# Max-pool-and-subtract on one core: 48 KB tiles in four buffers, the last one in three shrinking pieces, no ScalarE

## Chip, cores and metric

The kernel runs on one core of a Trainium2 chip; the other cores are idle. The metric is the device time of one execution in microseconds (us); lower is better. A verdict of "same" means within 2%.

## The reference

```python
def setup_inputs():
    B, C, H, W = 8, 64, 256, 256
    return {"x": np.random.randn(B, C, H, W).astype(np.float32)}

def reference(x):
    ...   # pH = pW = 8
    x_r = x.reshape(B, C, oH, pH, oW, pW)
    pooled = x_r.max(axis=(3, 5))
    upsampled = np.repeat(np.repeat(pooled, pH, axis=2), pW, axis=3)
    return (x - upsampled).astype(np.float32)
```

From each 8 x 8 window its maximum is subtracted. 134.22 MB go in and 134.22 MB come out; each element is used once. In the kernels a "row" is 8 image lines of one channel, 2048 floats (8 KB) in one partition. 128 such rows, one per partition, are 1 MB, and "a tile of R rows" has R of them in each partition; the whole input is 128 rows deep.

## The kernel before

```python
    R = 2
    data_pool = ctx.enter_context(tc.tile_pool(name="data_pool", bufs=8))
    small_pool = ctx.enter_context(tc.tile_pool(name="small_pool", bufs=4))
    for i in range(ntiles):                      # 64 tiles
        dat = data_pool.tile([P, R, row_len], mybir.dt.float32, name="dat")
        nc.sync.dma_start(out=dat..., in_=src)   # load, cut here
        for r in range(R):
            nc.vector.tensor_reduce(out=pooled[:, r], in_=in_v, axis=XY, op=max)
        nc.scalar.activation(out=rep..., in_=pooled...to_broadcast(...), func=Copy)
        for r in range(R):
            nc.vector.tensor_tensor(out=dat_v, in0=dat_v,
                in1=rep[:, r].unsqueeze(1).to_broadcast([P, pH, W]), op=subtract)
        nc.scalar.dma_start(out=dst, in_=dat...)  # store
```

(Abridged.) Loads are issued from SP (queue q1), stores from the ScalarE sequencer (queue q10). A scheduler decided the order of instructions on each engine.

Of the kernel before, what the change touches and what calls it, by code (L numbers as in the profile page):

```python
# [1 line left out]

# [4 lines left out]


@with_exitstack  # L10
def kernel(
    ctx: ExitStack,
    tc: tile.TileContext,
    x: bass.AP,
    out: bass.AP,
):
    nc = tc.nc
    P = nc.NUM_PARTITIONS

    B, C, H, W = x.shape  # L20
    pH = pW = 8
    oH, oW = H // pH, W // pW

    x_rows = x.rearrange("b c (oh ph) w -> (b c oh) (ph w)", ph=pH)
    out_rows = out.rearrange("b c (oh ph) w -> (b c oh) (ph w)", ph=pH)
    n_rows = x_rows.shape[0]
    row_len = x_rows.shape[1]

    R = 2
    rows_per_tile = P * R  # L30
    ntiles = n_rows // rows_per_tile
    assert n_rows % rows_per_tile == 0

    data_pool = ctx.enter_context(tc.tile_pool(name="data_pool", bufs=8))
    small_pool = ctx.enter_context(tc.tile_pool(name="small_pool", bufs=4))

    for i in range(ntiles):
        dat = data_pool.tile([P, R, row_len], mybir.dt.float32, name="dat")
        src = x_rows[i * rows_per_tile : (i + 1) * rows_per_tile].rearrange(
            "(p r) d -> p (r d)", r=R  # L40
        )
        nc.sync.dma_start(out=dat.rearrange("p r d -> p (r d)"), in_=src)  # L42

        pooled = small_pool.tile([P, R, oW], mybir.dt.float32, name="pooled")
        rep = small_pool.tile([P, R, W], mybir.dt.float32, name="rep")

        for r in range(R):
            in_v = dat[:, r].rearrange("p (ph ow pw) -> p ow ph pw", ph=pH, ow=oW, pw=pW)
            nc.vector.tensor_reduce(  # L49
                out=pooled[:, r],  # L50
                in_=in_v,
                axis=mybir.AxisListType.XY,
                op=mybir.AluOpType.max,
            )

        nc.scalar.activation(  # L56
            out=rep.rearrange("p r (ow pw) -> p (r ow) pw", pw=pW),
            in_=pooled.rearrange("p r ow -> p (r ow)").to_broadcast([P, R * oW, pW]),
            func=mybir.ActivationFunctionType.Copy,
        )  # L60

        for r in range(R):
            dat_v = dat[:, r].rearrange("p (ph w) -> p ph w", ph=pH)
            nc.vector.tensor_tensor(  # L64
                out=dat_v,
                in0=dat_v,
                in1=rep[:, r].unsqueeze(1).to_broadcast([P, pH, W]),
                op=mybir.AluOpType.subtract,
            )

        dst = out_rows[i * rows_per_tile : (i + 1) * rows_per_tile].rearrange(
            "(p r) d -> p (r d)", r=R
        )
        nc.scalar.dma_start(out=dst, in_=dat.rearrange("p r d -> p (r d)"))  # L74


# [1 line left out]
_INS = ['x']  # L78
_OUTS = [((8, 64, 256, 256), 'float32')]


# [23 lines left out]
```

## Time and profile before

| | before |
|---|---|
| time, median of 3 runs | 631.79 us (631.71 to 631.91) |
| span of the profiled run | 630.3 us |
| VectorE (DVE) busy | 564.7 us, 90% |
| ScalarE (ACT) busy | 39.5 us, 6% |
| mean DMA rate | 426 GB/s |

Parts of the page of the kernel before: span, busy time, the DMA rows of the 40 time slices (busy tenths, then GB/s), the queues, the chain of waits, and the three large groups of instructions. A group's columns are line, engine, operation, output and input, count, then busy us and mean ns of one, then the idle time just before and what ended it.

```profile
span 630.3 us, 730 instructions
...
DVE 564.7 (90%) x256; ACT 39.5 (6%) x65; POOL 0.2 (0%) x4
...
DMA  9999999999999999999999999999999999999997
GB/s 361 418 433 433 432 431 432 428 431 433 431 428 433 432 432 433 433 431 432 431 429 431 433 432 428 432 432 431 433 433 431 433 429 429 431 433 433 431 405 334
...
q1 hardware_dynamic: 9216, 134.22, 50.0%
q10 hardware_dynamic: 9216, 134.22, 49.8%
...
DMA 81%; DVE 16%; issue 1%; DVEq 0%; ACT 0%; SPq 0%; ACTq 0%
...
L49 DVE TENSOR_REDUCE pooled<-dat 128x32 f32<-128x2048 f32 x128 | 285.0, 2276 | 57.6 <-DMA dat<-in_x_dram 57.6
L64 DVE TENSOR_TENSOR dat<-dat,rep 128x2048 f32<-128x2048 f32 x128 | 283.9, 2282 | 0.8 <-ACT rep L56 0.8
L56 ACT ACTIVATE rep<-pooled 128x512 f32<-128x512 f32 x64 | 38.2, 624 | 578.4 <-DMA dat<-in_x_dram 408.2
```

The DMA engines are full from end to end at about 431 GB/s; the two queues take half of them each. VectorE is busy for 90% and its only idle time of note is waiting for loads. ScalarE hardly delays anybody (0.8 us). What the engines do not use is at the two ends. The end of the kernel before, in windows of 4 us (us, DVE busy, ACT, POOL, clock, DMA share, GB/s), and then VectorE's instructions there (start, busy us, line, operation, count, idle before). A packet is counted in the window in which it starts, so a share can exceed 1.

```profile
608.00:612.00 4.00, 4.00 (x3) 0.00 (x0) 0.00 (x0) 1.00 0.78 332
612.00:616.00 4.00, 4.00 (x3) 0.00 (x0) 0.00 (x0) 1.00 1.07 455
616.00:620.00 4.00, 3.25 (x2) 0.63 (x1) 0.00 (x0) 1.00 0.95 406
620.00:624.00 4.00, 3.13 (x2) 0.00 (x0) 0.00 (x0) 1.00 0.47 201
624.00:628.00 4.00, 0.00 (x0) 0.00 (x0) 0.00 (x0) 1.00 1.08 459
```

```profile
604.60 2.29 DVE L49 TENSOR_REDUCE pooled<-dat 128x32 f32<-128x2048 f32 x1 [2.80 <-DMA dat<-in_x_dram]
606.80 8.88 DVE L64 TENSOR_TENSOR dat<-dat,rep 128x2048 f32<-128x2048 f32 x4
615.61 2.28 DVE L49 TENSOR_REDUCE pooled<-dat 128x32 f32<-128x2048 f32 x1
618.64 4.49 DVE L64 TENSOR_TENSOR dat<-dat,rep 128x2048 f32<-128x2048 f32 x2 [0.76 <-ACT rep L56]
```

VectorE gets the last tile at 604.6. It still has two earlier tiles to finish besides, so from 608 to 624 the store queue runs dry twice: a bubble of about 3 us.

### The profile page before, as it was taken

To read this page: it belongs to the slowest core of one execution; us is meant where nothing else is said; L and a number is where in the kernel's file an instruction comes from. 1 tells how busy PE (TensorE), PEld (TensorE's weight loads), DVE (VectorE), ACT (ScalarE), POOL (GpSimd) and SP (SyncE) were. 2 spreads that over 40 slices of the span, in tenths; PEclk is the share of its full clock that TensorE was granted. 3 is DMA by queue.
4 is the path that set the end of the run, shared out by engine and by line. 5 is a ranking of instruction groups with operands and counts; after the bars stand their busy time and mean duration, and the time that the engine had idled before them with its cause. 6 is when DMAs were issued, how large, how long until landed. Compare 5 with 4: busy or idle time off the path is not lost.

```text
span 630.3 us, 730 instructions
## 1 busy us (share of the span) xinstructions
DVE 564.7 (90%) x256; ACT 39.5 (6%) x65; POOL 0.2 (0%) x4
## 2 busy tenths in 40 slices
DVE  4999999889889889889889898898998988988985
ACT  1000010010000000000001001001001001001000
POOL 0000000000000000000000000000000000000000
DMA  9999999999999999999999999999999999999997
GB/s 361 418 433 433 432 431 432 428 431 433 431 428 433 432 432 433 433 431 432 431 429 431 433 432 428 432 432 431 433 433 431 433 429 429 431 433 433 431 405 334
DMA packets 18437, 268.48 MB, mean 426 GB/s; under 512 B 2048, under 2 KB 2048, under 8 KB 2048
## 3 DMA queue, kind: packets, MB, share of 16 engines
q1 hardware_dynamic: 9216, 134.22, 50.0%
q10 hardware_dynamic: 9216, 134.22, 49.8%
q14 instruction: 5, 0.04, 0.0%
HBM read 134.22 MB, written 134.22 MB: 426 GB/s over the span
## 4 chain that ended last, share of the span: by engine, by line
DMA 81%; DVE 16%; issue 1%; DVEq 0%; ACT 0%; SPq 0%; ACTq 0%
DMA dat<-in_x_dram 49%; DMA out_dram<-dat 32%; DVE dat L64 9%; DVE pooled L49 7%; DVEq L100 0%; ACT rep L56 0%; SPq L42 0%; ACTq L74 0%; DVEq L64 0%; ACTq L56 0%
## 5 line engine op out<-in xcount | busy, mean ns | idle before, releaser
L49 DVE TENSOR_REDUCE pooled<-dat 128x32 f32<-128x2048 f32 x128 | 285.0, 2276 | 57.6 <-DMA dat<-in_x_dram 57.6
L64 DVE TENSOR_TENSOR dat<-dat,rep 128x2048 f32<-128x2048 f32 x128 | 283.9, 2282 | 0.8 <-ACT rep L56 0.8
L56 ACT ACTIVATE rep<-pooled 128x512 f32<-128x512 f32 x64 | 38.2, 624 | 578.4 <-DMA dat<-in_x_dram 408.2
L56 ACT ACT_TABLE_LOAD x1 | 1.3, 1283 | 0.7 <-PEq L89 0.7
L89 POOL MEMSET const-uint8-127<- 128x1 uint8 x1 | 0.1, 103 | 0.0
L89 POOL MEMSET const-bfloat16-1.0<- 128x1 bf16 x1 | 0.1, 102 | 0.0
L89 POOL MEMSET const-float32-0.0<- 128x1 f32 x1 | 0.1, 99 | 0.2 <-issue 0.2
L89 POOL MEMSET const-float32-1.0<- 128x1 f32 x1 | 0.1, 99 | 0.0
## 6 DMA issues: line engine op xcount, KB each, us to landing
dat<-in_x_dram SPq DMA_DIRECT2D x64, 2048.0 KB, 29.6
out_dram<-dat ACTq DMA_DIRECT2D x64, 2048.0 KB, 19.0
```

Of the source, the lines that this page charges most:

```text
L49: nc.vector.tensor_reduce(out=pooled[:, r], in_=in_v, axis=mybir.AxisListType.XY, op=mybir.AluOpType.max,)
L56: nc.scalar.activation(out=rep.rearrange("p r (ow pw) -> p (r ow) pw", pw=pW), in_=pooled.rearrange("p r ow -> p (r ow)").to_broadcast([P, ...
L64: nc.vector.tensor_tensor(out=dat_v, in0=dat_v, in1=rep[:, r].unsqueeze(1).to_broadcast([P, pH, W]), op=mybir.AluOpType.subtract,)
L89: nc = _bacc.Bacc("TRN2", target_bir_lowering=False, num_devices=1)
```

## The change

Its intent: fewer and longer transfers (48 KB per partition instead of 16), less fixed cost per instruction (one reduction per tile, the subtraction reads the maxima directly), and a short end (the last tile comes in pieces of 3, 2 and 1 rows, so that little work is left after the last byte arrives). The order is that of the program. The core of the diff:

```diff
+TILES = [[2]] + [[6]] * 20 + [[3, 2, 1]]
+BUFS = 4
 ...
-        for r in range(R):
-            nc.vector.tensor_reduce(out=pooled[:, r], in_=in_v, ...)
-        nc.scalar.activation(out=rep..., in_=pooled...to_broadcast(...), func=Copy)
+            nc.vector.tensor_reduce(                      # one for all R rows
+                out=tops, in_=wins.rearrange("p r ph ow pw -> p r ow ph pw"), ...)
         for r in range(R):
             nc.vector.tensor_tensor(
-                in1=rep[:, r].unsqueeze(1).to_broadcast([P, pH, W]),
+                in1=tops[:, r].unsqueeze(1).unsqueeze(3).to_broadcast([P, pH, oW, pW]),
 ...
+    ctx.enter_context(tc.manual_schedule())
+    for pieces in TILES:
+        dat = data.tile([P, size * ROW], F32, name="dat")
+        for R in pieces:
+            src = x_rows[at : at + P * R].rearrange("(p r) d -> p (r d)", r=R)
+            dst = out_rows[at : at + P * R].rearrange("(p r) d -> p (r d)", r=R)
+            part = dat[:, done * ROW : (done + R) * ROW]
+            ...
+            nc.sync.dma_start(out=part, in_=src)
+        for part, tops, dst, R in parts:
+            pool_and_subtract(part, tops, R)
+            nc.scalar.dma_start(out=dst, in_=part)
```

More of the change, by code (lines that the diff above doesn't have):

```diff
@@ L7 @@
 from concourse._compat import with_exitstack
+F32 = mybir.dt.float32
+ROW = 2048
+TILES = [[2]] + [[6]] * 20 + [[3, 2, 1]]
+BUFS = 4
 @with_exitstack
@@ L21, with pool_and_subtract @@
     pH = pW = 8
-    oH, oW = H // pH, W // pW
+    oW = W // pW
     x_rows = x.rearrange("b c (oh ph) w -> (b c oh) (ph w)", ph=pH)
     out_rows = out.rearrange("b c (oh ph) w -> (b c oh) (ph w)", ph=pH)
-    n_rows = x_rows.shape[0]
-    row_len = x_rows.shape[1]
-    R = 2
-    rows_per_tile = P * R
-    ntiles = n_rows // rows_per_tile
-    assert n_rows % rows_per_tile == 0
-    data_pool = ctx.enter_context(tc.tile_pool(name="data_pool", bufs=8))
-    small_pool = ctx.enter_context(tc.tile_pool(name="small_pool", bufs=4))
-    for i in range(ntiles):
-        dat = data_pool.tile([P, R, row_len], mybir.dt.float32, name="dat")
-        src = x_rows[i * rows_per_tile : (i + 1) * rows_per_tile].rearrange(
-            "(p r) d -> p (r d)", r=R
-        )
-        nc.sync.dma_start(out=dat.rearrange("p r d -> p (r d)"), in_=src)
-        pooled = small_pool.tile([P, R, oW], mybir.dt.float32, name="pooled")
-        rep = small_pool.tile([P, R, W], mybir.dt.float32, name="rep")
-        for r in range(R):
-            in_v = dat[:, r].rearrange("p (ph ow pw) -> p ow ph pw", ph=pH, ow=oW, pw=pW)
+    assert sum(map(sum, TILES)) * P == x_rows.shape[0]
+    size = max(map(sum, TILES))
+    data = ctx.enter_context(tc.tile_pool(name="data", bufs=BUFS))
+    small = ctx.enter_context(tc.tile_pool(name="small", bufs=BUFS))
+    def pool_and_subtract(dat, tops, R):
+        wins = dat.rearrange("p (r ph ow pw) -> p r ph ow pw", r=R, ph=pH, ow=oW)
+        tops = tops.rearrange("p (r ow) -> p r ow", r=R)
+        if R == 1:
             nc.vector.tensor_reduce(
-                out=pooled[:, r],
-                in_=in_v,
+                out=tops[:, 0],
+                in_=wins[:, 0].rearrange("p ph ow pw -> p ow ph pw"),
                 axis=mybir.AxisListType.XY,
@@ L54 @@
             )
-        nc.scalar.activation(
-            out=rep.rearrange("p r (ow pw) -> p (r ow) pw", pw=pW),
-            in_=pooled.rearrange("p r ow -> p (r ow)").to_broadcast([P, R * oW, pW]),
-            func=mybir.ActivationFunctionType.Copy,
-        )
+        else:
+            nc.vector.tensor_reduce(
+                out=tops,
+                in_=wins.rearrange("p r ph ow pw -> p r ow ph pw"),
+                axis=mybir.AxisListType.XY,
+                op=mybir.AluOpType.max,
+            )
         for r in range(R):
-            dat_v = dat[:, r].rearrange("p (ph w) -> p ph w", ph=pH)
             nc.vector.tensor_tensor(
-                out=dat_v,
-                in0=dat_v,
-                in1=rep[:, r].unsqueeze(1).to_broadcast([P, pH, W]),
+                out=wins[:, r],
+                in0=wins[:, r],
+                in1=tops[:, r].unsqueeze(1).unsqueeze(3).to_broadcast([P, pH, oW, pW]),
                 op=mybir.AluOpType.subtract,
             )
-        dst = out_rows[i * rows_per_tile : (i + 1) * rows_per_tile].rearrange(
-            "(p r) d -> p (r d)", r=R
-        )
-        nc.scalar.dma_start(out=dst, in_=dat.rearrange("p r d -> p (r d)"))
+    ctx.enter_context(tc.manual_schedule())
+    at = 0
+    for pieces in TILES:
+        dat = data.tile([P, size * ROW], F32, name="dat")
+        pooled = small.tile([P, size * oW], F32, name="pooled")
+        parts = []
+        done = 0
+        for R in pieces:
+            src = x_rows[at : at + P * R].rearrange("(p r) d -> p (r d)", r=R)
+            dst = out_rows[at : at + P * R].rearrange("(p r) d -> p (r d)", r=R)
+            part = dat[:, done * ROW : (done + R) * ROW]
+            tops = pooled[:, done * oW : (done + R) * oW]
+            parts.append((part, tops, dst, R))
+            at += P * R
+            done += R
+            nc.sync.dma_start(out=part, in_=src)
+        for part, tops, dst, R in parts:
+            pool_and_subtract(part, tops, R)
+            nc.scalar.dma_start(out=dst, in_=part)
 _INS = ['x']
```

## The prediction

> **What bounds it now.** The DMA engines. In the page's slices DMA is at 9 in all but the last, at 428 to 433 GB/s from the third to the thirty-eighth. Every byte is needed, so at 431 GB/s moving alone takes 268.44 MB / 431 = 622.8 us of the 630.3 us span.[...] VectorE is second: 256 instructions (groups: mean 2276 and 2282 ns), 564.7 us busy, 4.4 us per row of 1 MB against 4.85 us of DMA for that row in and out. The chain (DMA 81%) alternates 29 us loads and 19 us stores: queueing behind busy engines, so shorter waits for buffers gain nothing.
>
> About 7.5 us isn't moving: 2.3 us until data flows, 1.5 us after the last byte, and a bubble of about 3 us at the end. In windows of 4 us the rate falls to 332 GB/s at 608 and 201 GB/s at 620: loads are over, and VectorE, two tiles behind, releases the last three stores at 611, 616 and 623 us.
>
> **What the change does.**
> - 128 DMAs of 2 MB become 48, most of 6 MB, in runs of 48 KB instead of 16 KB. Packets now are 16 KB and take about 0.61 us (queue table: 50.0% of 16 engines' span over 9216 packets, 1024 of them tiny)[...]. If runs are cut to 16 KB again, the gain is zero.
> - ScalarE's 64 copies (39.5 us, off the path; VectorE waited 0.8 us on them) vanish: under 1 us.
> - 128 reductions become 24; the fixed part of one is about 0.06 us, so VectorE saves about 6 us, off the path. Subtractions read maxima with step 0 inside; I expect 2.28 us still.
> - Coarser tiles: load 29, compute 26.4, store 29 us, together 85, against four tiles x 29 = 116 us per turn of buffers. Queues never run dry.
> - Start: the first tile is as before; 20 rows are requested up front instead of 16. No loss.
> - End: pieces of 3, 2, 1 rows; VectorE finishes the last row 4.4 us after it lands, while earlier pieces still drain. The 3 us bubble shrinks to about 0.5.
>
> **Sum.** 631.8 - 2.5 (end)[...] - 0.5 = 625.8 us. Range 623.2 to 629.4. Faster by over 2% needs 619.2[...]: 2%. Slower by over 2%: 3%.
>
> **What would show it.** Slices flat at 431 to 435 GB/s; far fewer packets, of 48 KB; the last slice above 370 GB/s; subtractions of 2.28 us; six-row reductions near 12.9 us; VectorE near 560 us; no wait of the load queue that takes DMA under 9.
>
> **What would make it wrong.** Subtractions over 2.6 us (VectorE would bind); packets still of 16 KB and 431 GB/s (then 628.5); a store queue dry early, or large store packets starving the small last loads, a bubble of several us.

The sum came to 625.8 us. One term is cut out of it, 3 us less for the longer packets (the author's estimate of 4 us, at three chances in four); the terms left give 628.8. The fixed 0.06 us of a reduction is what the traces show: 2.195 us from one reduction to the next before, less 2.133 us per further row within one after ("Why the prediction was wrong").

## The result

Here and below, a ratio is the mean time of one kernel's fast runs over the mean of the other's of the same rounds, so it is not quite the ratio of the medians quoted.

| | before | changed |
|---|---|---|
| median | 631.85 us (4 runs) | 631.81 us (4 runs) |
| lowest to highest | 631.71 to 631.91 | 630.37 to 634.03 |
| ratio | | 1.0004, 95% interval 0.9981 to 1.0027 |

No gain. The median lies above the predicted range, which ended at 629.4, and 6 us above the predicted 625.8. New is the scatter: before, runs agree within 0.2 us; after, they spread over 3.7 us, all at full clock.

The same parts of the page of the changed kernel (the groups are those with different shapes kept apart):

```profile
span 629.1 us, 305 instructions
...
DVE 560.0 (89%) x152; POOL 0.2 (0%) x4
...
DMA  9999999999999999999999999999999999999995
GB/s 383 430 403 450 444 406 444 450 406 444 447 406 447 444 409 447 447 406 447 444 416 438 447 419 434 447 428 425 447 431 422 444 438 422 444 419 430 439 423 252
...
q1 hardware_dynamic: 3456, 134.22, 49.6%
q10 hardware_dynamic: 3456, 134.22, 49.4%
...
another core or an unknown queue 51%; DVE 26%; DMA 19%; issue 1%; SPq 1%
...
dat<-in_x_dram SPq DMA_DIRECT2D x1, 1024.0 KB, 64.9
```

```profile
L55 DVE TENSOR_TENSOR dat<-dat,pooled 128x2048 f32<-128x2048 f32 x128 | 284.0, 2286 | 0.8
L48 DVE TENSOR_REDUCE pooled<-dat 128x192 f32<-128x12288 f32 x20 | 259.0, 12950 | 40.7 <-DMA dat<-in_x_dram 40.7
...
L41 DVE TENSOR_REDUCE pooled<-dat 128x32 f32<-128x2048 f32 x1 | 2.3, 2285 | 7.1 <-DMA dat<-in_x_dram 7.1
```

Much is as foreseen: VectorE has 560.0 us, subtractions take 2286 ns and six-row reductions 12.95 us, ScalarE has no work left, there are 3456 packets per queue instead of 9216. (The swing between 403 and 450 GB/s is how packets of 48 KB fall into slices of 15.7 us: 8 or 9 of them started per engine would make 400 or 450 GB/s, an estimate.) The half of the chain that names an unknown queue is not another core, since only one runs; the page could not match that DMA. Two lines do not fit. The last slice is at 252 GB/s where 370 was expected, and the last load of 1 MB took 64.9 us from issue to landing, with VectorE idle 7.1 us for it. The end, as for the kernel before (these windows have no ACT column):

```profile
608.00:612.00 4.00, 0.52 (x1) 0.00 (x0) 1.00 1.00 424
612.00:616.00 4.00, 0.42 (x1) 0.00 (x0) 1.00 0.99 426
616.00:620.00 4.00, 3.96 (x2) 0.00 (x0) 1.00 0.93 397
620.00:624.00 4.00, 0.19 (x1) 0.00 (x0) 1.00 0.72 299
624.00:628.00 4.00, 0.00 (x0) 0.00 (x0) 1.00 0.10 41
```

```profile
599.57 4.42 DVE L48 TENSOR_REDUCE pooled<-dat 128x64 f32<-128x4096 f32 x1 [2.96 <-DMA dat<-in_x_dram]
604.03 4.49 DVE L55 TENSOR_TENSOR dat<-dat,pooled 128x2048 f32<-128x2048 f32 x2
615.58 2.29 DVE L41 TENSOR_REDUCE pooled<-dat 128x32 f32<-128x2048 f32 x1 [7.06 <-DMA dat<-in_x_dram]
617.90 2.29 DVE L55 TENSOR_TENSOR dat<-dat,pooled 128x2048 f32<-128x2048 f32 x1
```

Most of the data is out by 624, which is 4 to 5 us sooner than before; yet the span ends at 629.1. In the window from 624 to 628 only 41 GB/s flow, about what one or two of the 16 DMA engines move (27.2 GB/s each by the packet durations below). So some engines were still at work when the others were done.

The trace shows this directly. Every DMA ends with 16 four-byte writes (1024 such packets for 64 DMAs on each queue before), called completion writes here. In the records of one engine, chained below, exactly one of them follows the eight data packets that this engine moves for a DMA (8 x 16 engines are the 128 partitions), and VectorE starts on the last load only after the last of its 16 (604.60 after 604.1 before, 615.58 after 615.2 changed). So each is read here as one engine's sign that its part is done. Sorted by time and taken by sixteens, they tell when the median engine and when the slowest engine finished (us from the start of the span, as in the profile; the first data packet starts at 1.7):

```
                        last load            last store
                     median  slowest       median  slowest
before                602.0    604.1        629.0    629.1
changed               609.7    615.2        623.7    628.0
changed, second run   lag 5.3               lag 4.3
```

("Lag" is slowest less median; the second run is the one of experiment 4.) The median engine gained 5.3 us, as hoped. The slowest engine trails by 4.3 us at the end, by 5.5 us at the last load, and the last row waits for the slowest (615.2; VectorE starts it at 615.58).

A packet, here and below, is one record of the trace: the bytes that one DMA moves for one partition, or one completion write. Durations give a clean law, by median: 8 KB takes 309 ns, 16 KB 611, 24 KB 912, 32 KB 1213, 40 KB 1514, 48 KB 1815. From 8 to 48 KB that is 1506 ns for 40,960 bytes, 27.2 GB/s per engine or 435 GB/s for 16, plus about 8 ns per packet. Data packets alone therefore take, per engine, 16384 x 611 / 16 = 625.7 us before and 619.9 us after (the same sum over its four lengths): 5.8 us less. The gain exists, and is lost elsewhere.

The records do not name their engine, but they can be chained: on one engine each record begins 3 to 4 ns before the one ahead of it ends. From the completion write that comes last in the changed kernel's trace (628.0), exactly one record fits at every step back to 207.0 us, 296 records without a gap. So the slowest engine never idles in that time. It is late because 13 of its packets each took over 50 ns more than the median of their length, 3.7 us together, where it trails by 4.3; the other slow packets lie on other engines or before 207 us. On it, packets of the two queues alternate one by one, 8 KB loads with 48 KB stores at the end: with the completion writes counted, the queue changes at each of the 271 steps up to the last load's completion write; where one queue comes twice in a row, the other's completion write had taken a turn between.

### The profile page after: what moved, and what is told of

It is laid out like the page before. It is cut to its first block, busy times and chain, and to the rows that moved or that the text cites. A ratio compares the mean times of both kernels' runs of the same rounds, so it can differ in the third digit from the quotient of the medians.

```text
span 629.1 us, 305 instructions
## 1 busy us (share of the span) xinstructions
DVE 560.0 (89%) x152; POOL 0.2 (0%) x4
## 3 DMA queue, kind: packets, MB, share of 16 engines
q1 hardware_dynamic: 3456, 134.22, 49.6%
q10 hardware_dynamic: 3456, 134.22, 49.4%
## 4 chain that ended last, share of the span: by engine, by line
another core or an unknown queue 51%; DVE 26%; DMA 19%; issue 1%; SPq 1%
DVE pooled L48 13%; DVE dat L55 13%; DMA dat<-in_x_dram 12%; DMA out_dram<-dat 8%; SPq L77 1%; DVE pooled L41 0%
## 5 line engine op out<-in xcount | busy, mean ns | idle before, releaser
L48 DVE TENSOR_REDUCE pooled<-dat 128x192 f32<-128x12288 f32 (+2 forms) x23 | 274.4, 11930 | 52.3 <-DMA dat<-in_x_dram 52.3
L55 DVE TENSOR_TENSOR dat<-dat,pooled 128x2048 f32<-128x2048 f32 x128 | 284.0, 2286 | 0.8
L41 DVE TENSOR_REDUCE pooled<-dat 128x32 f32<-128x2048 f32 x1 | 2.3, 2285 | 7.1 <-DMA dat<-in_x_dram 7.1
## 6 DMA issues: line engine op xcount, KB each, us to landing
dat<-in_x_dram SPq DMA_DIRECT2D x1, 1024.0 KB, 64.9
```

Of the source, the lines that this page charges most:

```text
L41: nc.vector.tensor_reduce(out=tops[:, 0], in_=wins[:, 0].rearrange("p ph ow pw -> p ow ph pw"), axis=mybir.AxisListType.XY, op=mybir.AluOp ...
L48: nc.vector.tensor_reduce(out=tops, in_=wins.rearrange("p r ph ow pw -> p r ow ph pw"), axis=mybir.AxisListType.XY, op=mybir.AluOpType.max,)
L55: nc.vector.tensor_tensor(out=wins[:, r], in0=wins[:, r], in1=tops[:, r].unsqueeze(1).unsqueeze(3).to_broadcast([P, pH, oW, pW]), op=mybir ...
```

## The experiments

Two theories were formed. **A**: the shrinking pieces hurt. Each engine takes packets from the two queues in turn, one each, whatever their length (in the chain above the turn changes with every record), so load packets of 24, 16 and 8 KB fall behind store packets of 48 KB. **L/S**: with packets of 48 KB some engines lag by chance, and a program that ends tightly pays for the slowest one. Rivals: the pieces are needed; the lag is an accident; it comes from large DMAs or from the layout in HBM rather than from packets. All fifteen experiments gave correct results. "Slow packets" below are those of more than 50 ns over the median of their length, after the first 50 us, counted in the one trace of each run; by the chain above they are most of what makes an engine lag in the changed kernel.

### 1. The last tile whole (e1)

```diff
-TILES = [[2]] + [[6]] * 20 + [[3, 2, 1]]
+TILES = [[2]] + [[6]] * 21
```

> Undoes the shrinking pieces: a last tile of 6 rows, loaded and stored whole. Theory A (the pieces hurt: their small load packets of 24, 16 and 8 KB take turns with 48 KB store packets, so the last row lands about 10 us later than a fair share would give): the last load lands near 583 us for most engines, VectorE ends near 610 us, the store queue is never dry for more than 2 us, and the time is the same as the changed kernel or up to 3 us shorter. Rival B (the pieces are what saves the end: without them nobody stores while VectorE works 26 us on the last tile): about 10 to 20 us longer, 640 to 650 us.

Measured: median 630.0 us, 629.24 to 635.44; ratio to before 0.9983 (0.9959 to 1.0006). Rival B is out: giving the pieces up costs nothing at all. The profile fell on the slowest run: one engine trailed by 9.8 us at a store near the end, the last load landed at 585.2 for the median and 590.1 for the slowest engine, VectorE started the last tile late and DMA ran nearly dry from 608 to 616:

```profile
608.00:612.00 4.00, 4.00 (x2) 0.00 (x0) 1.00 0.09 37
612.00:616.00 4.00, 4.00 (x3) 0.00 (x0) 1.00 0.03 12
```

So "never dry for more than 2 us" missed in that run. The lag is one part of it (VectorE waited 3.69 us before the last tile); the rest is that a tile stored whole has nothing to store while VectorE works 26 us on it.

### 2. The last tile loaded whole, stored in pieces (e2)

```diff
-        for R in pieces: ... nc.sync.dma_start(out=part, in_=src)      # three loads
+        nc.sync.dma_start(out=dat[:, : total * ROW], in_=src)          # one load
         # pooling, subtraction and store stay in pieces of 3, 2, 1 rows
```

> Last tile loaded in one 6-row DMA, pooled, subtracted and stored in pieces of 3, 2, 1 rows. Theory A: no starved load and the store queue never dry, so the time is 1.5 to 4 us under the changed kernel (628 to 630), what remains over 625 being engines that lag. Rival B: as the changed kernel within 1 us.

Measured: five fast runs of 627.53 to 630.62 us, mean 629.2, and one of 637.46, which counts as slow (over 1.5% above the fastest) and is left out; ratio to before 0.9960 (0.9943 to 0.9976), beside 1.0002 (0.9981 to 1.0023) for the changed kernel in the same rounds. So one edit in the last tile's load is worth 631.9 - 629.2 = 2.7 us, give or take 1.7 by the two intervals. The run left out was at full clock too and may be the lag itself; counted in, the mean is 630.6 and the gain 1.3 us. The profile is of the 627.53 run, the fastest. Its last rows on VectorE and its last windows:

```profile
606.95 2.28 DVE L41 TENSOR_REDUCE pooled<-dat 128x32 f32<-128x2048 f32 x1
609.26 2.29 DVE L55 TENSOR_TENSOR dat<-dat,pooled 128x2048 f32<-128x2048 f32 x1
```

```profile
616.00:620.00 4.00, 0.00 (x0) 0.00 (x0) 1.00 0.99 424
620.00:624.00 4.00, 0.00 (x0) 0.00 (x0) 1.00 0.68 287
624.00:628.00 4.00, 0.00 (x0) 0.00 (x0) 1.00 0.01 2
```

The last tile lands at 582.7 (slowest engine 584.5). VectorE finishes the last row at 611.6, without a wait, instead of 620.2, 13 us before the engines are done with the stores; DMA is full to the end, and here the slowest engine was only 1.8 us late. Theory A holds: the late last row is gone.

### 3. The same code with tiles of 2 rows (e3)

```diff
-TILES = [[2]] + [[6]] * 20 + [[3, 2, 1]];  BUFS = 4
+TILES = [[2]] * 64;  BUFS = 12
```

> The changed kernel's code and program order, but every tile of 2 rows in 12 buffers, so packets of 16 KB. Theory P (fixed cost of about 8.5 ns per packet): packets take 611 ns again and the steady rate falls back to 431 GB/s, packet time about 627 us per engine, time 631 to 634 us. Rival (the packets are not what changed the rate, the order is): 433 GB/s or more with 16 KB packets, under 630 us.

Measured: 630.91 us, 630.72 to 630.94; ratio 0.9986 (0.9974 to 0.9998). Packets take 611 ns and the slices show 431 GB/s, as theory P has it, and the scatter is gone. The time just misses the expected 631 to 634. New code and program order without longer packets are worth about 0.9 us.

### 4. The changed kernel again (e4)

No edit.

> The changed kernel itself again. Theory L (some of the 16 DMA engines lag by a few us, by chance of the execution, and the last row waits for the slowest): runs scatter over 3 us or more again, mean near 631.8, with the slowest engine of the last load 4 us or more behind the median one in the trace. Rival (the lag of the first trace was an accident of one execution): runs within 1 us, and a lag under 2 us.

Measured: 629.42 to 633.94, median 631.98. Scatter and lag are back (5.3 us at the last load, 4.3 at the last store), with 40 slow packets of 48 KB against 37 in the first trace. In both traces of this kernel the slow ones are loads until about 550 us, and stores from there on, where small load pieces come in between (14 and 17 of them); without the load pieces, no store packet was slow in experiment 2 and five in all of experiment 1. So the pieces seem to add lag too.

### 5. Load pieces kept, but packets of one length at the end (e5)

```diff
+        small_runs = i >= len(TILES) - 4
-            src = x_rows[at : at + P * R].rearrange("(p r) d -> p (r d)", r=R)
+            lay = "(r p) d -> p r d" if small_runs else "(p r) d -> p r d"
+            src = x_rows[at : at + P * R].rearrange(lay, r=R)     # dst alike
```

> Keeps the load pieces of 3, 2, 1 rows, but moves the last four tiles in runs of 8 KB, loads and stores alike, so load and store packets near the end have one size. Theory A (small load packets starve beside 48 KB store packets): the last row lands at about 583 to 590 us on most engines instead of 609, VectorE has no wait of 7 us before the last row, and the slowest engine trails no more at the last load than three loads before it; 8 KB packets cost 309 ns against 1815/6 = 302.5, in all about 2.5 us, so about 630 us. Rival (three load DMAs are late whatever the packets): last row still lands after 605 us, time 634 us.

Measured: 638.26 us, 635.91 to 641.17: slower, where 630 was expected. The edit moved the collision instead of removing it. At the first of the four tiles, loads in 8 KB packets met two stores still in 48 KB packets:

```profile
528.25 12.95 DVE L48 TENSOR_REDUCE pooled<-dat 128x192 f32<-128x12288 f32 x1 [30.10 <-DMA dat<-in_x_dram]
```

That tile landed at 521.0, 2.5 us after the last store packet of 48 KB was gone (518.5; both on the median engine), and 54.5 us after the tile before it instead of 29: VectorE waited 30.10 us. Behind it, with equal packets, all six rows of the last tile had landed at 573.1 on the median engine (587.0 on the slowest) while VectorE worked on earlier tiles until 606.9, and VectorE had no wait before the last row, as theory A said. The time expected was wrong, and so was the expectation that the slowest engine would trail no more at the last load than three loads before: 13.8 us against 7.0. The turn-taking is shown in the large.

### 6. Six rows per DMA, in packets of 16 KB (e6)

```diff
# against experiment 2
-        src = x_rows[...].rearrange("(p r) d -> p (r d)", r=total)
+        src = x_rows[...].rearrange("(g p r) d -> p g (r d)", r=2, p=P)   # stores alike; pieces 2, 2, 2
```

> Tiles of 6 rows and the store pieces of the second experiment, but each DMA in runs of 16 KB. Theory S (the scatter and the lag belong to 48 KB packets): runs within 0.5 us of each other, few packets more than 50 ns slow (4 to 6 as with 2-row tiles, not 28 to 55), time 630 to 632 because packets take 611 ns. Rival T (they belong to the 6 MB DMAs and deep queues, not to the packet): scatter of 3 us or more stays.

Measured: 629.23 us, 629.22 to 629.45; ratio 0.9962 (0.9949 to 0.9975); 1 slow packet. Scatter 0.2 us with the same 6 MB DMAs, buffers and queue depth: rival T is out. It is also faster than foreseen; its engines lag 0.7 us at the end against 1.7 in experiment 3, which may account for 1 us of the 1.7 between the two; it was not tested further.

### 7 and 8. Three rows, four rows (e7, e8)

```diff
+TILES = [[2]] + [[3]] * 41 + [[2, 1]];  BUFS = 8        # experiment 7, 24 KB
+TILES = [[2]] + [[4]] * 31 + [[2]];     BUFS = 6        # experiment 8, 32 KB
```

Both load each tile whole, as in experiment 2.

> Tiles of 3 rows in 8 buffers, packets of 24 KB, last tile stored as 2 and 1 rows. Packets 912 ns, packet time per engine 625 to 626 us. Theory S: scatter between those of 16 and 48 KB, time 628 to 629. Rival T: scatter as small as with 2-row tiles.

> Tiles of 4 rows in 6 buffers, packets of 32 KB, last tile of 2 rows. Packets about 1213 ns, packet time per engine 623 to 624.5 us. If the gain of larger packets comes without much lag, 627 to 628 us with a scatter of about 1 us, the best version; if lag grows with packet size, 628 to 631 with a scatter of 2 us.

Measured: 628.96 us (628.78 to 629.15), ratio 0.9957, 4 slow packets; and 627.76 us (627.64 to 627.89), ratio 0.9937 (0.9925 to 0.9949), 2 slow packets. The packets took 912 and 1213 ns, as expected; their sums per engine, 624.7 and 622.7 us by the actual durations, fell just under the expected ranges. Lag does not grow gradually up to 32 KB: with scatters of 0.4 and 0.25 us both are about as steady as with 16 KB.

### 9. Shrinking pieces with packets of 32 KB (e9)

```diff
-TILES = [[2]] + [[6]] * 20 + [[3, 2, 1]]
+TILES = [[2]] + [[4]] * 30 + [[3, 2, 1]]      # otherwise the changed kernel
```

> The changed kernel with tiles of 4 rows (packets of 32 KB) and its last tile still loaded in pieces of 3, 2, 1 rows. If the two causes are separate, the lag is gone here (scatter about 0.3 us, as in the 4-row run) and the starved last load stays, milder because a 32 KB store packet holds a small load packet up less: the last row lands several us after VectorE has finished the piece before it, or just about then; 0.5 to 3 us over the 4-row kernel with whole loads, 628.2 to 630.8. Rival (the pieces only hurt through lagging engines): within 0.3 us of the 4-row kernel, 627.5 to 628.1.

Measured: 628.21 us (628.11 to 628.23), ratio 0.9947. That is 0.45 us over experiment 8 and 0.48 over experiment 12, at the very edge between the two expectations. VectorE waited 2.26 us before the last row instead of 7.06, but the store queue was still fed:

```profile
613.28 2.29 DVE L41 TENSOR_REDUCE pooled<-dat 128x32 f32<-128x2048 f32 x1 [2.26 <-DMA dat<-in_x_dram]
```

So starved pieces by themselves cost about half a microsecond here (experiments 8 and 12 also have six buffers of 4 rows where this one has four of 6, which was not tested apart); at 48 KB, where they also meet lagging engines, 2.7. This run is also the cleanest test of packet length: against the changed kernel only the tiles' rows differ, pieces and buffers stay, and the scatter falls from over 3.5 us to 0.1 and the time by 3.5 us (ratios 0.9947 and 1.0002).

### 10. Five rows (e10)

```diff
+TILES = [[3]] + [[5]] * 24 + [[3, 2]];  BUFS = 4        # 40 KB, loads whole
```

> Tiles of 5 rows in 4 buffers, packets of 40 KB, last tile loaded whole and stored as 3 and 2 rows. Packet time per engine about 622.9 us. If the lag sets in gradually with packet size: some 10 to 20 slow packets and a scatter of 1 to 2 us. If it sets in just above 32 KB: as with 48 KB, 25 or more slow packets and a scatter of 3 us or more. If it belongs to 48 KB alone: under 6 slow packets and a scatter under 0.5 us, 627.3 to 628.2.

Measured: 627.26 us (627.06 to 627.56), ratio 0.9932 (0.9920 to 0.9945): the best of all. 1 slow packet, lag 0.7 us. Its slices:

```profile
GB/s 369 401 429 453 427 430 443 427 430 443 427 432 440 428 432 438 430 438 435 427 438 438 425 435 440 425 435 440 425 438 440 422 440 438 422 446 432 422 448 349
```

The last slice is at 349 GB/s, where the changed kernel had 252.

### 11. The 48 KB layout in packets of 16 KB (e11)

```diff
# against experiment 2
-        nc.sync.dma_start(out=dat[:, : total * ROW], in_=src)
+        for c in range(0, total * ROW, 2 * ROW):           # stores alike; pieces 2, 2, 2
+            nc.sync.dma_start(out=dat[:, c : c + 2 * ROW], in_=src[:, c : c + 2 * ROW])
```

> Tiles of 6 rows laid out as in the changed kernel (48 KB of HBM from one partition to the next), but each moved by three DMAs of 16 KB per partition. If the lag comes from the 48 KB distance between partitions in HBM: slow packets (three per 48 KB, so some tens) and a scatter of 3 us. If it comes from the packet's length: under 10 slow packets, scatter under 0.5 us. Time 629 to 632 either way, since packets take 611 ns[...].

Measured: 630.53 us (630.33 to 630.71), 4 slow packets. Partitions 48 KB apart in HBM bring no lag; length of packet does.

### 12. Four rows, last tile stored row by row (e12)

```diff
# against experiment 8
-TILES = [[2]] + [[4]] * 31 + [[2]]
+TILES = [[2]] + [[4]] * 31 + [[1, 1]]
```

> The 4-row kernel with its last tile of 2 rows, still loaded whole, stored one row at a time. The store queue is not dry at the end of the 4-row run, so this should gain nothing: 627.5 to 628 us, scatter under 0.4 us. It also repeats the 4-row kernel beside the runs of this call. A gain of 0.5 us or more would say that a bubble was left.

Measured: 627.73 us (627.70 to 627.93), ratio 0.9940. No gain; nothing was left at the end to shorten.

### 13 to 15. What is it about 48 KB? (e13, e14, e15)

```diff
# in words, against experiment 2
+TILES = [[2]] + [[7]] * 17 + [[4, 3]];  BUFS = 3       # 13: 56 KB
+  each store cut into DMAs of at most 3 rows           # 14: loads 48 KB, stores 24 KB
+  each load cut into DMAs of at most 3 rows            # 15: loads 24 KB, stores 48 KB
```

> Tiles of 7 rows in 3 buffers, packets of 56 KB, last tile loaded whole and stored as 4 and 3 rows. Packets about 2115 ns. If lag sets in above 40 KB and stays: 20 or more packets over 50 ns slow after 50 us, a scatter of 2 us or more. If it belongs to 48 KB alone: under 6 slow packets and a scatter under 0.5 us. The time itself may be longer, since three buffers leave a turn of 34 + 31 + 34 us against 102 us: 628 to 640.

> Second experiment's kernel with each 6-row store cut into two DMAs of 24 KB per partition; loads keep 48 KB packets. If 48 KB load packets alone bring the lag: 20 or more slow packets in the load queue and a scatter of 2 us or more. If both queues must have 48 KB packets: under 6 slow, scatter under 0.5 us, 628 to 630.

> The mirror: loads cut into two DMAs of 24 KB per partition, stores keep 48 KB packets. Turns are one packet each, so loads get a third of the engines while both queues have work; loads may come late and VectorE wait, 628 to 645. If the lag is the loads' alone: under 6 slow packets. If store packets of 48 KB bring it too, as at the end of the changed kernel, where the slow ones were all stores: 15 or more slow packets in the store queue.

| | median us | lowest to highest | ratio to before | slow load / store packets |
|---|---|---|---|---|
| 13, 56 KB | 657.89 | 650.28 to 669.27 | 1.0375 | 408 / 260 |
| 14, loads 48, stores 24 | 627.54 | 626.73 to 631.45 | 0.9947 | 11 / 1 |
| 15, loads 24, stores 48 | 653.27 | 648.27 to 654.76 | 1.0328 | 348 / 213 |
| 2, both 48, for comparison | 630.08 | 627.53 to 637.46 | 0.9960 | 28 / 0 |

(That loads get "a third of the engines" in 15 was an estimate, 24 KB of 24 + 48 by the one-by-one turns of the chain in the changed kernel; it was not measured. The profile of 13 fell on its slowest run, which counts as slow, so its packet counts are those of a bad run; its fast runs are 650 us and more as well. The times of 13 and 15 lie above what was expected, 628 to 640 and 628 to 645.) Slowness is not peculiar to 48 KB: in these runs it sets in above 40 KB (1 slow packet in experiment 10, 28 in experiment 2) and is far worse at 56 KB (668), where three buffers may also have cost something. Long stores beside shorter loads are the bad mixture: both kinds of packet get slow, and the loads starve besides (VectorE waited 79.1 us for them, against 59.4 in the changed kernel). The slow packets of 15 lost 247 us over 16 engines, 15.5 us per engine; the profiled run is 16 us longer than the kernel before. Experiment 14 lies between its two expectations (11 slow packets, one run of four 4 us late): long loads beside shorter stores are milder, but not free of lag. This fits experiments 4 and 5, where the pieces put short loads beside 48 KB stores. Why a long packet stalls at all, no run here shows.

## Why the prediction was wrong

- **Bound by the DMA engines, VectorE second: right.** All that moved the time by more than 1 us were packets and queues.
- **Packets grow to 48 KB and their fixed part shrinks: right, and larger than said.** The author's estimate was 4 us; packet time fell by 5.8 us and the median engine was done 5.3 us sooner.
- **The sum's term of 3 us off for the larger packets failed.** It took the mean engine for the kernel: that every engine gets the shorter packet time was the step that did not hold. The last store is over when the slowest of 16 engines is, and with 48 KB packets that was 4.3 us after the median in both traces. Packets of 40 KB have nearly the same packet time (620.3 us per engine, from their counts) without lag, and from experiment 2 to experiment 10 the time fell from 629.2 to 627.3. So the lag cost about 2 us in the mean even after the end was mended, and nearly all of the scatter.
- **"End: ... the 3 us bubble shrinks to about 0.5": failed.** I wrote that VectorE finishes the last row 4.4 us after it lands, while earlier pieces still drain. It did take 4.6 us. But the row landed at 609.7 on the median engine, because packets of 24, 16 and 8 KB take turns with stores of 48 KB, and at 615.2 on the slowest, which lags besides. VectorE idled 7.06 us and issued the last store at 620.2. The prediction named "large store packets starving the small last loads" as a danger and gave it no weight. Loading the tile whole recovered 2.7 us, within 1.7 (experiment 2); the same pieces with steady 32 KB packets cost only 0.45 us (experiment 9), so most of the 2.7 probably came from starvation and lag together.
- **Coarser tiles keep the queues full, the start is as before, ScalarE is off the path: right.** Slices stay at 9, reductions take 12.95 us, and subtractions 2286 ns with the step-0 operand. (The 0.06 us per reduction agrees with the traces: before, four reductions start 2.195 us apart, 8.86 us in all; in one reduction each further row adds 2.133 us, 12.95 against 2.285. VectorE's busy time fell by 4.7 us, where about 6 was said.)
- **The account.** 631.9 (changed) less 2.7 (whole load) less 1.9 (no lag) is 627.3, the 5-row kernel. The two causes act together, so the shares depend on the order: shorter packets first give 3.5 us (experiment 9), and loading the tile whole then 0.5. The remaining 1.5 us to the predicted 625.8 are not settled.

Two things stay open: what makes packets over 40 KB stall, above all stores beside shorter loads; and how much of experiment 13's 26 us is due to its three buffers. Of the latter its trace tells a part: in that run, 37 us longer than the kernel before, slow packets lost 24.8 us per engine (397 us over 16), the longer packets saved about 6, and engines stood some 20 us longer without a packet.

## What to carry to other kernels

In this kernel, which DMA bounds at about 431 GB/s, longer runs per partition paid by saving a fixed cost of about 8 ns per packet, but look for the length at which the slowest engine starts to lag: here 32 to 40 KB gave the full gain (627.76 and 627.26 us), and 48 KB gave all of it back with the loads in pieces (631.81) and about half with them whole (mean 629.2). Queues took turns by packet (the last load of 1 MB, in 8 KB packets beside stores of 48 KB, took 64.9 us), so do not shrink the last loads while long stores are draining: load the last tile whole, and cut its compute and its stores instead. When runs of one kernel begin to scatter, compare the slowest engine with the median one before looking for a cause in the mean rate.
